# When the adaLN modulation halves end, who copies their result and when, and which engine makes two of their granules, in a one-core GLA + FNet layer

## The chip, the cores and the metric

The kernel runs on one core of a Trainium2 chip. The metric is device time in microseconds (us). Before the change the median of three runs is 1913.21 us (1912.01 to 1913.78).

The engines are named as the profile names them: PE is TensorE (PEld its weight loads), DVE is VectorE, ACT is ScalarE, POOL is GpSimd, SP is SyncE. Each takes its instructions in order from a queue of its own. A matmul writes to PSUM, and ScalarE or VectorE copy from there.

## The reference, cut to what matters

One inference step of one layer, on 128 context tokens and 256 latent tokens, 384 columns in all, with a model width of 2048:

```python
mod = silu(cond) @ w_ada + b_ada            # cond: c_ctx for context, c for latent tokens
sh1, sc1, ga1, sh2, sc2, ga2 = split(mod, 6)          # m = 0 .. 5
h = rmsnorm(x, norm_pre_mix) * (1 + sc1) + sh1
proj = h @ w_in                             # q | k | v | output gate | decay factors | Fourier channels
o = bidirectional_gla(q, k, v, decays)      # chunked scans, per-head RMSNorm, SiLU gate
f = real(fft2(fourier_channels))            # per group, over positions and channels
g_a, g_b = split(sigmoid(h @ w_gate + b_gate), 2)
m = (g_a * (o @ w_br_gla) + g_b * (f @ w_br_four)) @ w_out
x = x + ga1 * rmsnorm(m, norm_post_mix)
h = rmsnorm(x, norm_pre_ffn) * (1 + sc2) + sh2
x = x + ga2 * rmsnorm((silu(h @ w_ffn_gate) * (h @ w_ffn_up)) @ w_ffn_down, norm_post_ffn)
```

The change is about `mod` alone, and in it about m = 2, 3 and 4 (ga1, sh2, sc2), which are first needed late: ga1 in the output projection `w_out`, sh2 and sc2 behind it. There are only two condition vectors, so `mod` is a product of a 2048 x 2 matrix with very large weights, 2048 columns for each m.

## The kernel before

**Matmuls.** All is fp32. A weight tile of 128 x 1024 comes by a DMA of SP's queue (`raw`), and is then split into a high part `whi` (a cast, ScalarE, in `split`, L275) and a low part `wlo` (`raw` minus `whi`, VectorE, L295). The data are split likewise (`A_hi`, `A_lo`; `split_act`, L385, with VectorE's half in L387). `gemm` (L330; its matmul is L334) then issues 24 matmuls for one weight tile: for each of eight 128-row blocks the products `A_hi`·`whi`, `A_lo`·`whi` and `A_hi`·`wlo`, 128x384 each, into the PSUM tile `pmm`. Weight tiles for the Fourier channels are first folded by two VectorE operations into `ws` (L248, L249).

**The order on each engine** is the order in which the Python program emits instructions; nothing is rearranged around the change. Beside the main loops run generators, each advanced by one `yield` after every gemm (`step`, L326). One gemm with what is emitted behind it is called a step. The stages, in order:

- *GLA stage*: the projections q and k and the gates of `w_gate` (`proj`, L356, two steps each). `side()` of L1013 advances the GLA generator `gl` (L819: its matmuls write `dl`, `po` and others through L828, its states are `S`) and then the modulation generator.
- *Fourier stage* (`run_after`, L1093): modulation only at three turns.
- *Output-gate units* (`proj` with `gcol`, L1234, which gives `gs`, then `o`): `side()` of L1220 advances modulation at some turns, then the second Fourier transform (its PSUM tiles are `pp` and `pe`, its split results `edT` and `d`), then the Nyquist weights. Between units stand pieces of the Fourier branch projection, `four` (L1267), whose matmuls are `pf<-edT,whi` (L1281) and `pf<-edT,wlo` (L1282).
- *GLA branch projection*: for each i in `TAIL` one modulation step ahead of the gemm. Its end is `gate` times `pmm` (L1338).
- *w_out stage* (L1402 to L1433): 32 gemms with `wout` behind every second (squares and products into `qs`, by ScalarE and VectorE), modulation through `paced` (L374), which advances the generator as often as the sum of `rate[0]` passes a whole number; at `i == KT - 4` whatever is left is emitted at once. Behind this stage stand the row sums with `prow`, then the feed-forward network, which takes more than half of the time.

**Modulation.** m = 2, 3, 4 are made in six halves of 1024 columns by `ada_rest` (L730). A half has 16 granules, one for each block of 128 rows (the sixth leaves its last to the code behind `w_out`). Each granule is one step: POOL issues the load of a 128x1024 tile `adaw` (two buffers), and VectorE multiplies it by the two condition columns of `spad` and adds it into `adacc`, a tile of 2 x 1024 a partition, by two operations (L749; the first granule of a half, which has nothing to add to, by L747). Then the sum over the 128 partitions is taken on TensorE, the *selection*: `ada_select` (L722, matmul in L725), four matmuls for the first column and then four for the second, against a selector `selr`, into the PSUM tile `pr`. ScalarE copies `pr` to `adev` (L691). One step later two transposes (L695) turn it into `ptm`, and VectorE copies that into `mods` (L704) and adds the bias (L709), for some m multiplies too (L712).

A half's steps before the change: 16 granules, the last followed by one more empty `yield` (L757); then the selection and the copy to `adev`; then the transposes with VectorE's copies, and in the same step the first granule of the next half. That is 18 steps from half to half.

**Two granules on TensorE.** In the output-gate units turns 0 to 6 and turn 8 of `side()` carry a granule as described. At turns 9 and 13 the flag `on_pe` is set: there `ada_granule` (L716) makes the granule with four matmuls of its own (L718), straight from `adaw` and `spad` into `pr`, which is opened early for this and stays open until the half's selection, in the w_out stage.

Of the kernel before, what the change touches and what calls it, by code (L numbers as in the profile page):

```python
# [21 lines left out]
P = 128  # L22
# [16 lines left out]
XU = 1  # L39
GF = 25  # L40
GD = 256
TAIL = {4: False, 8: False, 10: False, 11: False, 13: False, 14: False}


C_TRI = 0
# [63 lines left out]
def tile_step(ctx: ExitStack, tc: tile.TileContext, a, o):  # L109
# [576 lines left out]

    adap = ctx.enter_context(tc.tile_pool(name="adap", bufs=1))

    def ada_tail(pr, m, half):
        ev = adap.tile([P, 256], F32, tag="adev", name="adev")  # L690
        ACT.copy(ev, pr)  # L691
        yield
        pt = pss.tile([P, 2, P], F32, tag="side", name="ptm")
        for b in range(2):
            PE.transpose(pt[:, b, :], ev[:, b * P : (b + 1) * P], ident)  # L695

        ada_out(DVE.tensor_copy, pt, m, half)
        ada_mods(m, half)

    def ada_out(copy, pt, m, half):  # L700
        src = pt.rearrange("p b (j r) -> p j b r", r=32)
        mh = mods[:, m, 8 * half : 8 * half + 8, :]
# [8 lines left out]
        if w1 is not None:  # L711
            DVE.tensor_mul(mh, mh, bc(norms[:, w1, :]))  # L712

    on_pe, ada_left = [False], []

    def ada_granule(pr, w, k, opened):  # L716
        for j in range(4):
# [10 lines left out]
                )  # L728

    def ada_rest(todo):  # L730
        for m, half in todo:
            acc = adap.tile([P, 2, 1024], F32, tag="adacc", name="adacc")
            pr, fresh = None, True
            final = (m, half) == todo[-1]
            for k in range(KT - final):
                w = adap.tile([P, 1024], F32, tag="adaw", name="adaw", bufs=2)
                POOL.dma_start(w, a["w_ada"][m - 2, half, k])
                if on_pe[0]:
                    opened = pr is not None
                    if not opened:  # L740
                        pr = pss.tile([P, 256], F32, tag="side", name="pr")
                    ada_granule(pr, w, k, opened)
                    yield
                    continue
                for c in range(2):
                    if fresh:
                        DVE.tensor_scalar_mul(acc[:, c, :], w, spad[:, k, c : c + 1])  # L747
                    else:
                        DVE.scalar_tensor_tensor(  # L749
                            acc[:, c, :], w, spad[:, k, c : c + 1], acc[:, c, :], op0=ALU.mult, op1=ALU.add,  # L750
                        )
                fresh = False
                yield
            if final:
                ada_left.append(acc)
                return
            yield  # L757
            opened = pr is not None
            if not opened:
                pr = pss.tile([P, 256], F32, tag="side", name="pr")  # L760
            ada_select(pr, acc, opened)
            yield from ada_tail(pr, m, half)

    def over_ends(k, t, r):

# [367 lines left out]
    with ExitStack() as s:  # L1133
# [85 lines left out]

        def side():  # L1220
            while True:
                on_pe[0] = turn[0] in (9, 13)
                if turn[0] < 7 or turn[0] in (8, 9, 13):
                    next(ada_gen, None)
                on_pe[0] = False
                turn[0] += 1
                next(df, None)
                next(nw, None)
                yield
# [72 lines left out]
        for b, i in mix_order:  # L1302
            if b == "o":
                if i == 1:
                    gate_of()
                proj(psm, hT, lambda p, i=i: gcol(p, i), sd, [lambda n=n: four(n) for n in between[i]])
                if i == 1:
                    gate_of()
                continue
            if b == "b":  # L1310
                if not i:
                    for g in (df, nw):
                        for _ in g:
                            pass
                    depth[0] = 4
                    spare_raws.extend([
                        lambda: px.tile([P, G], F32, tag="wr", name="raw3"), lambda: px.tile([P, G], F32, tag="cd", name="raw3"),
                    ])
                if not any(i in x for x in between):
                    four(i)  # L1320
            else:
                catch_up()
                if mT is None:
                    mT = alloc_A()
                if i == KT - 3:
                    depth[0] = 2
                    spare_raws.clear()
                if i in TAIL:
                    on_pe[0] = TAIL[i]
                    next(ada_gen, None)  # L1330
                    on_pe[0] = False
                p = psm.tile([P, T], F32, tag="mm", name="pmm")
                w = grab()
                while unstored:
                    unstored.pop()()
                gemm(p, w, oT, 8)
                g, y = gates.pop((b, i))
                DVE.tensor_mul(g, g, p)  # L1338
                DVE.tensor_add(y, y, g)
                if late:  # L1340
                    split_act(*late.pop())
                late.append((mT[0][:, i, :], mT[1][:, i, :], y))
                gate_of()
# [8 lines left out]
    with ExitStack() as s:  # L1352
# [44 lines left out]
            ACT.activation(sq2, mg32(i), AF.Square)  # L1397
            return sq0, pr, sq2

        rate[0] = 0.9  # L1400
        spare_h = {-4: ((pe, "hid_hi", 1), (pe, "hid_lo", 1)), -2: ((pe, "S0", 1), (pe, "S1", 1))}
        spare_w = ((adap, "adaw", 2), (adap, "adaw", 2))  # L1402
        for i in range(KT):
# [755 lines left out]
```

## Time and profile before

| what | value |
| --- | --- |
| median of three runs | 1913.21 us |
| the profiled execution, as timed | 1912.95 us |
| its span, first to last instruction | 1910.8 us |
| mean granted TensorE clock | 0.999 |
| ScalarE, GpSimd busy | 1002.2 us (52%), 82.7 us (4%) |
| HBM traffic over the span | 198 GB/s |

How to read the profile's lines: the first lists for each engine the busy time, its share of the span and the number of instructions. The chain of work that ended last is followed back from the last instruction, at each step to what released it; its line gives each engine's share. A line by stretches ("130.00:440.00") holds the length of the stretch, then busy time and instructions for PE, PEld, DVE, ACT and POOL, then the granted clock, the DMA share and GB/s. A line of the timeline holds the start in us, the time from the start of the first to the end of the last instruction in the group, the engine, the line of the code, the operation, what it writes and reads by the program's names, and how many; in square brackets the idle time of the engine before it, in us, and what ended it. Matmuls overlap in TensorE, so the next group can start before the last has ended. "issue" in the chain is time in which an engine waited for nothing that the profile shows.

### The profile page before, as it was taken

The numbers are of one execution on the slowest core, as the hardware profiler recorded it, in microseconds if no ns is written. First come the engines' busy times: TensorE is split into PE (matmuls) and PEld (weight loads), VectorE is DVE, ScalarE is ACT, GpSimd is POOL, SyncE is SP. The second block draws the span as 40 slices with busy tenths as digits, with TensorE's granted clock in tenths as the row PEclk, the third lists the DMA queues.
The fourth block names the chain that finished last, engine by engine and source line by source line (L and its number), as shares of the span: only waits on it lengthen the run. The fifth ranks groups of instructions, "written<-read, shape, count | busy, mean of one in ns | idle before, by whom it ended". The sixth has DMA issues, their size and how long they took to land.

```text
span 1910.8 us, 27279 instructions
## 1 busy us (share of the span) xinstructions
PE 1894.6 (99%) x10282; PEld 1675.1 (88%) x10282; DVE 1654.6 (87%) x2170; ACT 1002.2 (52%) x1430; POOL 82.7 (4%) x146
## 2 busy tenths in 40 slices
PE   8999999999999999999999999999999999999998
PEld 5679999999999999999988888888888888888886
DVE  5669897889969899998788989998999889997886
ACT  4235445444456654446456465646564656465644
POOL 0001111101000000004000000000000000000000
PEclk9999999999999999999999999999999999999999
DMA  9976766866657887666255656464646464746344
GB/s 390 400 278 232 262 225 225 274 205 211 216 176 233 278 288 260 206 219 221 67 186 152 188 147 202 135 213 116 223 129 219 119 219 116 232 106 199 95 159 138
DMA packets 237864, 389.70 MB, mean 204 GB/s; under 512 B 51188, under 2 KB 163924, under 8 KB 233380
## 3 DMA queue, kind: packets, MB, share of 16 engines
q1 hardware_dynamic: 218500, 330.02, 52.4%
q0 software_dynamic: 13952, 50.39, 8.6%
q10 hardware_dynamic: 5280, 7.55, 1.1%
q8 instruction: 81, 1.33, 0.3%
q14 instruction: 51, 0.42, 0.1%
HBM read 361.94 MB, written 16.78 MB: 198 GB/s over the span
## 4 chain that ended last, share of the span: by engine, by line
PE 95%; DMA 2%; DVE 2%; ACT 1%; issue 0%; SPq 0%; DVEq 0%; ACTq 0%
PE pmm L334 33%; PE pgu L346 31%; PE pdn L346 18%; PE pv L514 3%; PE pgm L497 1%; DMA slab<-in_w_ada 1%; PE pf L1281 1%; PE pfo L1083 1%; PE pmm L1561 1%; PE pf L1282 1%; PE po L828 1%; PE pfo L1084 0%; PE px L532 0%; DMA raw<-in_w_d 0%; DVE x1b L2016 0%; PE dl L828 0%
## 5 line engine op out<-in xcount | busy, mean ns | idle before, releaser
L334 PE MATMUL pmm<-A_hi,whi 128*128 128x384 f32 x1088 | 366.6, 337 | 0.0
L334 PE MATMUL pmm<-A_hi,wlo 128*128 128x384 f32 x1088 | 364.2, 335 | 0.1
L334 PE MATMUL pmm<-A_lo,whi 128*128 128x384 f32 x1088 | 363.9, 334 | 0.0
L1708 ACT CAST whi<-u 128x1024 fp32r<-128x1024 f32 x200 | 210.2, 1053 | 212.7 <-DVE u L1718 82.5
L1708 ACT CAST whi<-raw 128x1024 fp32r<-128x1024 f32 x175 | 184.0, 1051 | 169.7 <-DMA raw<-in_w_g 51.6
L1719 DVE TENSOR_TENSOR wlo<-u,whi 128x1024 fp32r<-128x1024 f32 x200 | 244.0, 1220 | 26.8 <-ACT whi L1708 21.4
L346 PE MATMUL pgu<-whi,A_lo 128*128 128x512 f32 x640 | 249.0, 389 | 0.0
L346 PE MATMUL pgu<-whi,A_hi 128*128 128x512 f32 x640 | 249.0, 389 | 0.0
L1719 DVE TENSOR_TENSOR wlo<-raw,whi 128x1024 fp32r<-128x1024 f32 x175 | 213.3, 1219 | 21.9 <-ACT whi L1708 12.3
L295 DVE TENSOR_TENSOR wlo<-raw,whi 128x1024 fp32r<-128x1024 f32 x161 | 196.2, 1219 | 29.6 <-ACT whi L308 29.1
L308 ACT CAST whi<-raw 128x1024 fp32r<-128x1024 f32 x147 | 154.3, 1050 | 123.5 <-DMA raw<-in_w_out 46.8
L749 DVE SCALAR_TENSOR_TENSOR adacc<-adaw,spad,adacc 128x1024 f32<-128x1024 f32 x174 | 215.3, 1278 | 0.7 <-DMA adaw<-in_w_ada 0.5
L334 PEld LDWEIGHTS pmm<-A_hi,whi 128*128 128x128 f32 x1088 | 204.2, 188 | 2.9 <-issue 1.7
L334 PEld LDWEIGHTS pmm<-A_hi,wlo 128*128 128x128 f32 x1088 | 204.2, 188 | 0.7 <-DVE wlo L295 0.6
L334 PEld LDWEIGHTS pmm<-A_lo,whi 128*128 128x128 f32 x1088 | 204.4, 188 | 0.2
L346 PE MATMUL pdn<-whi,hid_hi 128*128 128x512 f32 x480 | 186.8, 389 | 0.0
L346 PE MATMUL pdn<-whi,hid_lo 128*128 128x512 f32 x480 | 186.7, 389 | 0.0
L346 PE MATMUL pgu<-wlo,A_hi 128*128 128x512 f32 x640 | 184.0, 389 | 0.0
L346 PEld LDWEIGHTS pgu<-whi,A_lo 128*128 128x128 f32 x640 | 120.2, 188 | 25.0
L346 PEld LDWEIGHTS pgu<-wlo,A_hi 128*128 128x128 f32 x640 | 120.1, 188 | 25.0
L346 PEld LDWEIGHTS pgu<-whi,A_hi 128*128 128x128 f32 x640 | 120.1, 188 | 24.9
L346 PE MATMUL pgu<-whi,S 128*128 128x512 f32 x480 | 128.3, 389 | 0.0
(413 smaller groups left out, 3064.3 us busy)
## 6 DMA issues: line engine op xcount, KB each, us to landing
adaw<-in_w_ada POOLq DMA_DIRECT2D x95, 512.0 KB, 3.9
raw<-in_w_d SPq DMA_DIRECT2D x88, 512.0 KB, 3.9
slab<-in_w_ada SPq DMA_DIRECT2D x32, 1024.0 KB, 10.5
raw<-in_w_gate SPq DMA_DIRECT2D x64, 512.0 KB, 4.3
raw<-in_w_u SPq DMA_DIRECT2D x47, 512.0 KB, 3.8
raw<-in_w_in SPq DMA_DIRECT2D x46, 512.0 KB, 4.4
raw<-in_w_g SPq DMA_DIRECT2D x46, 512.0 KB, 3.6
u<-in_w_u SPq DMA_DIRECT2D x40, 512.0 KB, 4.5
```

The lines of the kernel that those rows point to most:

```text
L295: eng.tensor_sub(lo, raw, hi.bitcast(F32))
L308: ACT.copy(hi, raw)
L334: PE.matmul(dst, w[wi][:, k * n + n0 : k * n + n0 + P], x[xi][:, k0 + k, :], start=first and k == 0 and j == 0, stop=last and k == kts - 1 ...
L346: PE.matmul(dst, stat[x_][m], mov(w[w_], m), start=first and w_ == m == x_ == 0, stop=last and w_ == m == 1,)
L497: PE.matmul(pgv[q : q + 32, :], spad[:, k, :], slab[k // (KT // 2)][:, k % (KT // 2), :], start=k < 4, stop=k >= KT - 4,)
L514: PE.matmul(pv[2 * t + g], hT[x_][:, kb, t * P : (t + 1) * P], w_[:, g * 512 : (g + 1) * 512], start=kb == 0 and j == 0, stop=kb == KT - 1 ...
L749: DVE.scalar_tensor_tensor(acc[:, c, :], w, spad[:, k, c : c + 1], acc[:, c, :], op0=ALU.mult, op1=ALU.add,)
L828: PE.matmul(dst, w[wi], x[xi], start=first and j == 0, stop=last and j == 2)
L1083: PE.matmul(p, w_of[0][:, i, k, g, :], x[:, :, lo:hi], start=kt == 0, stop=False)
L1281: PE.matmul(pf[:, 0 : 2 * HT], w[0][:, c], x[k], start=k == 0, stop=False)
L1708: ACT.copy(hi, src)
L1719: DVE.tensor_sub(lo, src, hi.bitcast(F32))
```

## The change

1. **The halves end one step sooner.** The empty `yield` behind the 16th granule is gone: the selection and ScalarE's copy come one step after the last granule, at the place where the empty step was. So 17 steps lead from half to half, and each later half begins one step sooner than the one before.
2. **The copies come a step behind the transposes.** The transposes stay one step behind the selection, in the step of the next half's first granule. VectorE's copies into `mods` and the arithmetic on them are put into `finish()`, which is called one step later still, ahead of the next half's second granule.
3. **VectorE makes all granules.** Turns 9 and 13 of the output-gate units carry nothing, `on_pe` is gone, and so is the flag in `TAIL` (which was false throughout). `pr` is opened only at the selection. `ada_granule` stays for the last granule behind `w_out`. Since two steps fewer carry granules there and each half needs one step less, the places where later halves begin and end move by several steps.
4. **The pace in the w_out stage** is 0.85 instead of 0.9.

```diff
-TAIL = {4: False, 8: False, 10: False, 11: False, 13: False, 14: False}
+TAIL = (4, 8, 10, 11, 13, 14)
...
-    def ada_tail(pr, m, half):
-        ev = adap.tile([P, 256], F32, tag="adev", name="adev")
-        ACT.copy(ev, pr)
-        yield
-        pt = pss.tile([P, 2, P], F32, tag="side", name="ptm")
-        for b in range(2):
-            PE.transpose(pt[:, b, :], ev[:, b * P : (b + 1) * P], ident)
-
-        ada_out(DVE.tensor_copy, pt, m, half)
-        ada_mods(m, half)
...
     def ada_rest(todo):
+        finish = None
         for m, half in todo:
             acc = adap.tile([P, 2, 1024], F32, tag="adacc", name="adacc")
-            pr, fresh = None, True
             final = (m, half) == todo[-1]
             for k in range(KT - final):
                 w = adap.tile([P, 1024], F32, tag="adaw", name="adaw", bufs=2)
                 POOL.dma_start(w, a["w_ada"][m - 2, half, k])
-                if on_pe[0]:
-                    opened = pr is not None
-                    if not opened:
-                        pr = pss.tile([P, 256], F32, tag="side", name="pr")
-                    ada_granule(pr, w, k, opened)
-                    yield
-                    continue
+                if k and finish:
+                    finish()
+                    finish = None
                 for c in range(2):
-                    if fresh:
+                    if k == 0:
                         DVE.tensor_scalar_mul(acc[:, c, :], w, spad[:, k, c : c + 1])
...
-                fresh = False
                 yield
             if final:
                 ada_left.append(acc)
                 return
+            pr = pss.tile([P, 256], F32, tag="side", name="pr")
+            ada_select(pr, acc, False)
+            ev = adap.tile([P, 256], F32, tag="adev", name="adev")
+            ACT.copy(ev, pr)
             yield
-            opened = pr is not None
-            if not opened:
-                pr = pss.tile([P, 256], F32, tag="side", name="pr")
-            ada_select(pr, acc, opened)
-            yield from ada_tail(pr, m, half)
+            pt = pss.tile([P, 2, P], F32, tag="side", name="ptm")
+            for b in range(2):
+                PE.transpose(pt[:, b, :], ev[:, b * P : (b + 1) * P], ident)
+
+            def finish(pt=pt, m=m, half=half):
+                ada_out(DVE.tensor_copy, pt, m, half)
+                ada_mods(m, half)
...
         def side():
             while True:
-                on_pe[0] = turn[0] in (9, 13)
-                if turn[0] < 7 or turn[0] in (8, 9, 13):
+                if turn[0] < 7 or turn[0] == 8:
                     next(ada_gen, None)
-                on_pe[0] = False
...
                 if i in TAIL:
-                    on_pe[0] = TAIL[i]
                     next(ada_gen, None)
-                    on_pe[0] = False
...
-        rate[0] = 0.9
+        rate[0] = 0.85
```

**The first half's end, on TensorE.** In the GLA stage, between the gemms' matmuls, stand the two groups of `dl` for the two directions of the first head, and the selection (`pr<-adacc,selr`). Before:

```order
L334 MATMUL pmm<-A_hi,wlo 128x384
L828 MATMUL dl<-vr,part 128x256 x6
L334 MATMUL pmm<-A_hi,whi 128x384
...
L334 MATMUL pmm<-A_hi,wlo 128x384
L828 MATMUL dl<-vr,part 128x256 x6
L725 MATMUL pr<-adacc,selr 32x256 x8
L334 MATMUL pmm<-A_hi,whi 128x384
```

After, with the transposes into `ptm` (from `adev`) at the end:

```order
L334 MATMUL pmm<-A_hi,wlo 128x384
L818 MATMUL dl<-vr,part 128x256 x6
L714 MATMUL pr<-adacc,selr 32x256 x8
L334 MATMUL pmm<-A_hi,whi 128x384
...
L334 MATMUL pmm<-A_hi,wlo 128x384
L818 MATMUL dl<-vr,part 128x256 x6
L748 MATMUL ptm<-ident,adev 128x128 x2
L334 MATMUL pmm<-A_hi,whi 128x384
```

The selection has moved from behind the second group of `dl` to behind the first, one gemm of 24 matmuls sooner. Everything emitted ahead of it, on every engine, stands as before. The selections of the second, third and fourth half move by two, three and four steps in the same way.

**The output-gate units, on VectorE.** Here the first granules of the fifth half were made; `gs`, `o_lo`, `d` and `ws` are the unit's own. Before:

```order
L387 TENSOR_TENSOR o_lo<-gs,o_hi 128x384
L387 TENSOR_TENSOR d_5539<-pe,d_5539 128x194 x2
L248 TENSOR_TENSOR ws<-raw 128x512
L249 TENSOR_TENSOR ws<-raw 128x512
L704 COPY mods<-ptm 128x8 x2
L709 TENSOR_TENSOR mods<-mods,cols_b 128x16
L747 TENSOR_SCALAR adacc<-adaw,spad 128x1024 x2
L1240 SCALAR_TENSOR_TENSOR gs<-gs,gnorm,pt 128x384
L295 TENSOR_TENSOR wlo<-ws,whi 128x1024
```

After:

```order
L387 TENSOR_TENSOR o_lo<-gs,o_hi 128x384
L734 SCALAR_TENSOR_TENSOR adacc<-adaw,spad,adacc 128x1024 x2
L387 TENSOR_TENSOR d_5551<-pe,d_5551 128x194 x2
L248 TENSOR_TENSOR ws<-raw 128x512
L249 TENSOR_TENSOR ws<-raw 128x512
L734 SCALAR_TENSOR_TENSOR adacc<-adaw,spad,adacc 128x1024 x2
L1228 SCALAR_TENSOR_TENSOR gs<-gs,gnorm,pt 128x384
L295 TENSOR_TENSOR wlo<-ws,whi 128x1024
```

The fourth half's copies and the fifth's first granule have moved up and out of these rows, and two later granules of the fifth half stand there now.

**The fifth half's end, on VectorE.** In the w_out stage `qs`, `sq` and the 128x384 `pr` belong to `wout`. Before:

```order
L1388 TENSOR_TENSOR qs<-qs,sq 128x384
L749 SCALAR_TENSOR_TENSOR adacc<-adaw,spad,adacc 128x1024 x2
L295 TENSOR_TENSOR wlo<-raw,whi 128x1024
L749 SCALAR_TENSOR_TENSOR adacc<-adaw,spad,adacc 128x1024 x2
L295 TENSOR_TENSOR wlo<-raw,whi 128x1024
L1384 TENSOR_TENSOR qs<-qs,sq 128x384
L1386 TENSOR_TENSOR pr<-Bhi,Chi 128x384
L1387 TENSOR_TENSOR qs<-qs,pr 128x384
L1388 TENSOR_TENSOR qs<-qs,sq 128x384
L749 SCALAR_TENSOR_TENSOR adacc<-adaw,spad,adacc 128x1024 x2
L295 TENSOR_TENSOR wlo<-raw,whi 128x1024 x2
```

After:

```order
L1374 TENSOR_TENSOR qs<-qs,sq 128x384
L734 SCALAR_TENSOR_TENSOR adacc<-adaw,spad,adacc 128x1024 x2
L295 TENSOR_TENSOR wlo<-raw,whi 128x1024 x2
L1370 TENSOR_TENSOR qs<-qs,sq 128x384
L1372 TENSOR_TENSOR pr<-Bhi,Chi 128x384
L1373 TENSOR_TENSOR qs<-qs,pr 128x384
L1374 TENSOR_TENSOR qs<-qs,sq 128x384
L732 TENSOR_SCALAR adacc<-adaw,spad 128x1024 x2
L295 TENSOR_TENSOR wlo<-raw,whi 128x1024 x2
```

The fifth half's last granule, the lowest of the three before, is now the first row of its kind; the sixth half's first granule (L732) follows two steps behind. The selection on TensorE has moved up by three gemms.

More of the change, by code (lines that the diff above doesn't have):

```diff
@@ L712, in ada_mods @@
             DVE.tensor_mul(mh, mh, bc(norms[:, w1, :]))
-    on_pe, ada_left = [False], []
+    ada_left = []
     def ada_granule(pr, w, k, opened):
```

## The prediction

> **What bounds the kernel now.** I read the page first: the busy times, then the chain of work that ended last.
>
> ```profile
> PE 1894.6 (99%) x10282; PEld 1675.1 (88%) x10282; DVE 1654.6 (87%) x2170; ACT 1002.2 (52%) x1430; POOL 82.7 (4%) x146
> PE 95%; DMA 2%; DVE 2%; ACT 1%; issue 0%; SPq 0%; DVEq 0%; ACTq 0%
> ```
>
> TensorE (PE) is busy nearly throughout and makes up 95% of the chain. So the change can only act through TensorE: by work taken from it, or by a pause put into it. Next, busy times by stage, over the stretches in which modulation work is placed, and TensorE's waits in them.
>
> ```profile
> core 0: us, PE busy (x) PEld busy (x) DVE busy (x) ACT busy (x) POOL busy (x), PEclk, DMA share, GB/s
> 130.00:440.00 310.00, 310.00 (x1991) 305.39 (x1991) 269.93 (x339) 152.45 (x258) 34.11 (x67) 1.00 0.71 239
> 440.00:536.00 96.00, 95.90 (x644) 94.12 (x642) 89.21 (x132) 46.47 (x76) 5.94 (x11) 1.00 0.68 217
> 536.00:690.00 154.00, 154.00 (x975) 149.61 (x968) 130.39 (x239) 93.69 (x152) 5.30 (x10) 1.00 0.71 237
> 690.00:731.00 41.00, 41.00 (x244) 41.00 (x244) 40.59 (x60) 17.31 (x30) 2.65 (x5) 1.00 0.85 289
> 731.00:860.00 129.00, 129.00 (x756) 128.13 (x755) 117.73 (x139) 62.38 (x99) 10.07 (x19) 1.00 0.64 218
> PEld pmm L334 <- DVE wlo L295: 0.6, 2, 0.4
> ```
>
> TensorE has no idle stretch here, and its waits for VectorE's weight parts come to 0.6 us. VectorE (DVE) is the second fullest: 269.93 of 310 us in the first stretch and 40.59 of 41 in the fourth, so what it is given comes out late, though nobody waits for that now.
>
> **The first half's selection.** A modulation half is 16 granules on VectorE, then the selection on TensorE, then two transposes. Before, one empty step (a step is 24 matmuls of L334 and what is put behind them) stood between the last granule and the selection. It is gone: the selection moves to behind the first group of dl matmuls. Where it goes and what it waits for, from the timeline of VectorE and of TensorE, the price of a handover in the chain, and the granules' loads on the page:
>
> ```profile
> 210.71 2.48 DVE L749 SCALAR_TENSOR_TENSOR adacc<-adaw,spad,adacc 128x1024 f32<-128x1024 f32 x2
> 209.85 0.88 PE L828 MATMUL dl<-vr,part 128*128 128x256 f32 x6
> 210.57 0.34 PE L334 MATMUL pmm<-A_hi,whi 128*128 128x384 f32 x1
> 215.56 1.07 PE L725 MATMUL pr<-adacc,selr 128*32 128x256 f32 x16
> 216.56 0.45 PE L334 MATMUL pmm<-A_hi,whi 128*128 128x384 f32 x1
> 866.32 0.14 issue
> adaw<-in_w_ada POOLq DMA_DIRECT2D x95, 512.0 KB, 3.9
> ```
>
> The row at 210.71 is the last granule; it ends at 213.19. TensorE reaches the selection's new place at 210.57. The selection takes 1.00 us (215.56 to 216.56) in two parts: the first needs the granule's first operation, the second its second. Unhindered it would end at 211.57. As it is, the second part starts at 213.19 plus a handover of 0.14 (the chain's "issue" between VectorE's r and the matmuls of prow) and takes 0.50: end at 213.83, so **+2.3 us**. Bounds: 2.1 without the handover, 2.8 if the whole selection has to wait. Nothing on any engine is moved before this place, so these times stand. Behind the waiting selection TensorE's whole queue stands, the next 24 matmuls first; ScalarE's copy of the result stands behind a cast that waits for VectorE's S anyway. The granules' loads move with them on POOL's queue, the next one issued when a buffer of two comes free and landed 3.9 us later, within the step of 24 matmuls that lies between: 0, and without that cover the granule, and with it the selection, would come up to 3.9 us later. On SP's queue two neighbouring weight loads change places at the start of the output-gate units, with whole steps still ahead of their first use: 0.
>
> **The second, third and fourth.** Each half ends one step sooner than the last did, so the n-th last granule stands n-1 steps earlier and its selection n steps. At these places stand now:
>
> ```profile
> 291.15 2.47 DVE L749 SCALAR_TENSOR_TENSOR adacc<-adaw,spad,adacc 128x1024 f32<-128x1024 f32 x2
> 292.18 0.88 PE L828 MATMUL po<-part,qp 128*128 128x256 f32 x6
> 292.89 0.33 PE L334 MATMUL pmm<-A_hi,whi 128*128 128x384 f32 x1
> 369.14 2.47 DVE L749 SCALAR_TENSOR_TENSOR adacc<-adaw,spad,adacc 128x1024 f32<-128x1024 f32 x2
> 374.85 0.34 PE L334 MATMUL pmm<-A_hi,whi 128*128 128x384 f32 x1
> 534.10 2.47 DVE L749 SCALAR_TENSOR_TENSOR adacc<-adaw,spad,adacc 128x1024 f32<-128x1024 f32 x2
> 540.38 0.38 PE L1169 MATMUL pp<-cd,X 128*128 128x129 f32 x2
> ```
>
> Second: granule to 293.62, plus 0.64 gives 294.26, against 293.89 unhindered (292.89 + 1.00): **+0.4**. The pause before it moves both engines here; if VectorE follows less, nothing is left, and if it has its one additional granule not yet worked off, 2.5 more are due: bounds 0 and 2.9. Third: granule to 371.61, due at 374.85: 3.2 us of cover. Fourth: to 536.57, due at 540.38: 3.8 us. Both cost **0**; without that cover each would cost like the first. The waits of 0.6 us between 440 and 536 can vanish when TensorE comes later: **-0.3**, bounds 0 and -0.6.
>
> **The two granules of TensorE.** Rows around one of them, and the same place in a unit without:
>
> ```profile
> 602.67 0.34 PE L334 MATMUL pmm<-A_hi,wlo 128*128 128x384 f32 x1
> 602.94 0.64 PE L718 MATMUL pr<-adaw,spad 128*32 128x256 f32 x8
> 603.81 0.42 PE L1281 MATMUL pf<-edT,whi 128*128 128x388 f32 x1
> 616.90 0.34 PE L334 MATMUL pmm<-A_hi,wlo 128*128 128x384 f32 x1
> 617.32 0.42 PE L1281 MATMUL pf<-edT,whi 128*128 128x388 f32 x1
> ```
>
> From the last gemm matmul to pf it is 1.14 us with a granule and 0.42 without: 0.72 each, **-1.44** for both (the eight matmuls overlap: 0.64 us in all). VectorE pays in the same units. Its rows there, and the margin of a weight part:
>
> ```profile
> 573.56 0.68 DVE L249 TENSOR_TENSOR ws<-raw 128x512 f32<-128x512 f32 x1
> 576.03 0.24 DVE L704 COPY mods<-ptm 128x8 f32<-128x8 f32 x2 [1.79 <-PE ptm L695]
> 576.40 1.41 DVE L747 TENSOR_SCALAR adacc<-adaw,spad 128x1024 f32<-128x1024 f32 x2
> 601.40 1.22 DVE L295 TENSOR_TENSOR wlo<-ws,whi 128x1024 fp32r<-128x1024 f32 x1
> 604.08 0.25 PE L1282 MATMUL pf<-edT,wlo 128*128 128x194 f32 x1
> 688.37 0.56 DVE L1338 TENSOR_TENSOR gate<-gate,pmm 128x384 f32<-128x384 f32 x1 [0.77 <-PE pmm L334]
> ```
>
> Between ws and the next gs, the wait for ptm (1.79), the copies and the half-price first granule (576.03 to 577.81) become one granule of 2.48, with another of 2.48 ahead of d: from 574.24, 3.57 us become about 4.8, so VectorE is some 1.25 us later from here. wlo is done at 602.62 and used at 604.08: 1.46 us of margin, which the lateness (1.25) and TensorE's earliness (0.72) together exceed. So part of the 1.44 is waited away in these units; not all before 688.37, where VectorE's 0.77 us of idleness absorbs some lateness.
>
> **The fifth selection** settles what is left of it. It moves three steps up, to behind the matmuls that end before this row:
>
> ```profile
> 746.95 2.48 DVE L749 SCALAR_TENSOR_TENSOR adacc<-adaw,spad,adacc 128x1024 f32<-128x1024 f32 x2
> 747.02 0.33 PE L334 MATMUL pmm<-A_hi,whi 128*128 128x384 f32 x1
> ```
>
> Last granule to 749.43, plus 0.64: 750.07, against 748.02 unhindered: **+2.05**. This end is VectorE's: whatever TensorE gained before, it waits here that much longer, since VectorE at 99% from 690 to 731 does not follow. So of the -1.44 I count 0 (bounds 0 and -1.44), and VectorE's own shift, from -0.8 (688.37's idleness used up) to +1.25, I take at +0.2. ACT's copy behind this selection fills idle time. The rate of 0.85 for 0.9 only sets which steps carry granules; the last of them end about a step earlier than now, behind TensorE's matmuls: 0. Copying mods a step later removes waits of VectorE alone: 0; without spare VectorE time they would be worth 1.79 here.
>
> Sum: 2.3 + 0.4 - 0.3 + 2.05 + 0.2 = **+4.6 us** on the profiled execution's 1912.95 (span 1910.8), that is 1917.6; it lies 0.26 under the median of 1913.21, so 1917.8 for a median. Bounds: 2.1 + 0 - 0.6 + 1.9 - 0.8 = 2.6 and 2.8 + 2.9 + 2.2 + 1.25 = 9.2; the upper needs every worst at once, and I end my own case at +6.8: 1915.8 to 1920.0.
>
> What a pause does to the clock: the end of the trace.
>
> ```profile
> 1901.52 1.13 PE L2005 MATMUL py<-ep,psums 128*128 128x128 f32 x8 [1.82 <-ACT r L1981]
> 1903.36 1.06 PE L2005 MATMUL py<-ep,psums 128*128 128x128 f32 x8
> 1900.00:1905.00 5.00, 2.90 (x24) 2.73 (x24) 4.59 (x19) 3.34 (x9) 0.20 (x1) 1.00 0.75 219
> 1905.00:1911.00 6.00, 0.00 (x0) 0.00 (x0) 1.48 (x5) 0.00 (x0) 0.00 (x0) 0.62 0.58 167
> ```
>
> A pause of 1.82 us left the granted clock at 1.00. After the last matmul (to 1904.42) it fell: a mean of 0.62 over 6 us is full speed for 1.4 us and half after, a fall at 1906.4, some 2.0 us into the idleness. My pauses of 2.1 to 2.5 lie just above both, so the rows allow a drop. [...]
>
> **The rivals.** *VectorE is in time* (not slower): decided at 210.57, 292.89 and 747.02, where it would have to be 2.3, 0.4 and 2.05 us earlier against TensorE than reckoned. For it: its waits for ptm go. Against: nothing is moved ahead of the first place. Then only the granules count: -1.44, 1911.8. *VectorE becomes the bound*: its lateness of 1.25 in the output-gate units is not worked off and the second selection meets the additional granule; decided by the margin of 1.46 us at 604.08. For it: 40.59 of 41. Against: 0.77 idle at 688.37. Then +2 to +3 more: 1920 to 1921. *The clock drops in the pauses*: half speed for at least the 2 us that it took to fall costs 1 us or more each, two pauses 2 to 4: 1920 to 1922. It is decided by a pause over 2.0 us.
>
> **How the numbers follow.** My case 0.73, VectorE in time 0.12, VectorE the bound 0.10, the clock 0.05. Predicted 1917.8. The range 1914.8 to 1920.6 leaves out the first rival, the upper ends of the others and little of my case. What a measurement of this kernel can tell from no change is about 0.2%, 3.8 us: 1909.4 to 1917.0. Over it: most of my case and the two later rivals, 0.58. Within: the rest of my case and the first rival, 0.39. Under 1909.4 nothing leads: 0.03.
>
> **What would show it.** In the changed profile: before the first and fifth selections' second parts TensorE idle by about 2 us each, released by VectorE's adacc; under 1 us at the second, none at the third and fourth; no L718 between 560 and 680, and pf 0.72 sooner behind gemm; the gain gone by 760. Wrong would be: no idle time before selr matmuls, idle time before wlo of more than 2 us in all, or a granted clock under 1.00 before 1900.

## The result and the profile after

The changed kernel takes 1924.64 us (median of 6 runs, 1922.74 to 1928.13) against 1912.91 us before (6 runs, 1912.01 to 1913.78). The ratio is 1.0065, 95% interval 1.0052 to 1.0078: slower by 11.7 us, where 4.6 were forecast. Its profiled execution was the slowest of the six, 1928.13 us with a span of 1926.4. The six fall into groups by their granted clock: 1922.74 at 0.999, 1924.39 to 1927.36 at 0.997 and 0.998, 1928.13 at 0.996. So there is something in it that does not happen each time, and it shows in the clock.

The chain of work that ended last, and the stretches that were shown of before:

```profile
PE 86%; DVE 7%; DMA 3%; issue 1%; ACT 1%; SPq 0%; DVEq 0%; ACTq 0%
core 0: us, PE busy (x) PEld busy (x) DVE busy (x) ACT busy (x) POOL busy (x), PEclk, DMA share, GB/s
130.00:440.00 310.00, 306.67 (x1953) 300.99 (x1953) 270.06 (x335) 147.35 (x250) 35.57 (x70) 0.99 0.71 237
440.00:536.00 96.00, 95.34 (x586) 94.62 (x586) 90.38 (x134) 47.74 (x77) 5.92 (x11) 1.00 0.69 216
536.00:690.00 154.00, 151.82 (x991) 145.68 (x990) 129.53 (x231) 91.57 (x149) 4.75 (x9) 1.00 0.70 229
690.00:731.00 41.00, 41.00 (x247) 41.00 (x247) 39.78 (x66) 20.85 (x36) 1.58 (x3) 1.00 0.88 284
731.00:860.00 129.00, 125.81 (x720) 124.17 (x719) 110.23 (x133) 54.21 (x88) 10.04 (x19) 0.97 0.63 215
```

VectorE has gone from 2% of the chain to 7%: TensorE now waits for it. TensorE stands idle for 3.3 us in the first stretch and for 3.2 in the last, where it had no idle time before, and in these same two stretches the clock is below 1.00. In the output-gate units (536 to 690) it is idle for 2.2 us.

The first half's last granule on VectorE, the selection on TensorE (now L714), and the matmuls behind it:

```profile
212.09 2.48 DVE L734 SCALAR_TENSOR_TENSOR adacc<-adaw,spad,adacc 128x1024 f32<-128x1024 f32 x2
209.81 0.87 PE L818 MATMUL dl<-vr,part 128*128 128x256 f32 x6
213.48 0.64 PE L714 MATMUL pr<-adacc,selr 128*32 128x256 f32 x8 [2.79 <-issue]
214.62 1.08 PE L714 MATMUL pr<-adacc,selr 128*32 128x256 f32 x8 [0.51 <-DVE adacc L734]
215.63 0.69 PE L334 MATMUL pmm<-A_hi,whi 128*128 128x384 f32 x1
216.12 0.52 PE L334 MATMUL pmm<-A_lo,whi 128*128 128x384 f32 x1
220.60 0.44 PE L334 MATMUL pmm<-A_hi,whi 128*128 128x384 f32 x1
220.88 0.34 PE L334 MATMUL pmm<-A_lo,whi 128*128 128x384 f32 x1
```

There are two losses here. TensorE is done with `dl` at 210.68 and has the selection behind it at 215.70: 5.02 us for 1.00 us of work, 4.0 more than unhindered. Of these, 3.30 us are idle time (2.79 and 0.51); the rest is the selection itself, whose two parts no longer overlap and whose second part takes 1.08 us instead of 0.64. And the matmuls behind it take 0.52 us each instead of 0.34, until 220.6. The granted clock over these stretches, and over the same of the fifth half:

```profile
213.50:214.00 0.50, 0.50 (x8) 0.13 (x8) 0.50 (x1) 0.00 (x0) 0.00 (x0) 0.99 0.89 344
214.00:220.50 6.50, 5.99 (x27) 5.07 (x24) 5.24 (x9) 1.62 (x3) 0.53 (x1) 0.50 0.87 316
220.50:221.00 0.50, 0.50 (x3) 0.50 (x3) 0.12 (x1) 0.00 (x0) 0.00 (x0) 0.68 0.00 0
760.00:760.50 0.50, 0.14 (x4) 0.00 (x0) 0.50 (x1) 0.00 (x0) 0.00 (x0) 0.63 0.00 0
760.50:766.50 6.00, 5.80 (x23) 4.99 (x24) 2.51 (x3) 1.31 (x2) 0.53 (x1) 0.50 0.62 206
```

The clock (third number from the end) is at 0.50 from 214.0 to 220.8 and from 760.1 to 767.0. The fifth selection looks like the first, and the chain in order of time shows what the half clock costs: 24 matmuls of L334 in another unit, then those behind the fifth selection.

```profile
759.51 0.64 PE L714 MATMUL pr<-adacc,selr 128*32 128x256 f32 x8 [2.64 <-DVE adacc L734]
760.70 1.08 PE L714 MATMUL pr<-adacc,selr 128*32 128x256 f32 x8 [0.56 <-DVE adacc L734]
642.58 4.20 PE pmm L334 x24
761.78 6.75 PE pmm L334 x24
```

6.75 instead of 4.20: 2.55 us at each of the two places. In the output-gate units TensorE waits for VectorE's weight parts and for `o_lo`; the longest two:

```profile
612.63 0.36 PE L1270 MATMUL pf<-edT,wlo 128*128 128x194 f32 x1 [1.06 <-DVE wlo L295]
660.92 0.45 PE L334 MATMUL pmm<-o_lo,whi 128*128 128x384 f32 x1 [0.74 <-DVE o_lo L387]
```

How far the same matmuls of TensorE have shifted between the two profiled executions:

| matmul | before | after | shift |
| --- | --- | --- | --- |
| first `po` behind the first selection | 220.83 | 227.41 | 6.6 |
| a `pt` early in the output-gate units | 575.83 | 583.21 | 7.4 |
| a `pf` at their end | 651.72 | 661.38 | 9.7 |
| first row sum behind the w_out stage | 860.80 | 876.78 | 16.0 |

So 6.6 us are lost at the first selection, 0.8 from there to the units (0.2 of it at the second selection), 2.3 in the units and 6.3 at the fifth selection.

### The profile page after: what moved, and what is told of

Same layout as the page of the kernel before. It is cut to its first block, busy times and chain, and to the rows that moved or that the text cites. A ratio compares the mean times of both kernels' runs of the same rounds, so it can differ in the third digit from the quotient of the medians.

```text
span 1926.4 us, 27259 instructions
## 1 busy us (share of the span) xinstructions
PE 1901.8 (99%) x10266; PEld 1679.7 (87%) x10266; DVE 1659.2 (86%) x2174; ACT 1002.7 (52%) x1430; POOL 82.4 (4%) x146
## 4 chain that ended last, share of the span: by engine, by line
PE 86%; DVE 7%; DMA 3%; issue 1%; ACT 1%; SPq 0%; DVEq 0%; ACTq 0%
PE pgu L346 31%; PE pmm L334 26%; PE pdn L346 18%; PE pv L514 3%; DVE adacc L734 2%; DVE wlo L295 1%; PE pgm L497 1%; DMA slab<-in_w_ada 1%; PE pmm L1547 1%; PE pfo L1073 1%; PE pf L1269 1%; PE po L818 1%; PE px L532 0%; DMA raw<-in_w_br_gla 0%; DMA raw<-in_w_d 0%
## 5 line engine op out<-in xcount | busy, mean ns | idle before, releaser
L334 PE MATMUL pmm<-A_hi,whi 128*128 128x384 f32 x1088 | 369.0, 339 | 0.0
L334 PE MATMUL pmm<-A_hi,wlo 128*128 128x384 f32 x1088 | 366.1, 336 | 0.7 <-DVE wlo L295 0.7
L334 PE MATMUL pmm<-A_lo,whi 128*128 128x384 f32 x1088 | 365.8, 336 | 0.0
L734 DVE SCALAR_TENSOR_TENSOR adacc<-adaw,spad,adacc 128x1024 f32<-128x1024 f32 x178 | 220.2, 1278 | 0.8 <-DMA adaw<-in_w_ada 0.5
L334 PEld LDWEIGHTS pmm<-A_hi,whi 128*128 128x128 f32 x1088 | 205.8, 189 | 3.7 <-issue 3.3
L334 PEld LDWEIGHTS pmm<-A_hi,wlo 128*128 128x128 f32 x1088 | 205.6, 189 | 1.4 <-DVE wlo L295 1.3
L334 PEld LDWEIGHTS pmm<-A_lo,whi 128*128 128x128 f32 x1088 | 206.0, 189 | 0.2
```

Source lines behind the costliest of these rows:

```text
L334: PE.matmul(dst, w[wi][:, k * n + n0 : k * n + n0 + P], x[xi][:, k0 + k, :], start=first and k == 0 and j == 0, stop=last and k == kts - 1 ...
L734: DVE.scalar_tensor_tensor(acc[:, c, :], w, spad[:, k, c : c + 1], acc[:, c, :], op0=ALU.mult, op1=ALU.add,)
```

## The experiments

Theory A: what is lost is the two waits at the first and the fifth selection, and the half clock behind each. Theory B: the two granules that VectorE took over make it the bound, and the waits only show it. Each kernel was timed in turns with the kernel before, whose medians are 1913.07 us beside the first four kernels below, 1913.30 beside the next three and the last, and 1913.41 beside the three on the length of a wait.

### The empty step back in every half

Of the kernel after, VectorE making all granules, the copies a step late:

```diff
+            yield
             pr = pss.tile([P, 256], F32, tag="side", name="pr")
             ada_select(pr, acc, False)
...
-        rate[0] = 0.85
+        rate[0] = 0.97
```

> The kernel after, with the empty step restored between the last granule and the selection of every half (pace in the w_out stage 0.97, since two granules more are left for it). Theory A (TensorE waits at the first and fifth selection, 4.1 and 3.7 us, and each wait is followed by some 6.5 us at half clock, 2.5 us more): both waits and the half clock go, granted clock 0.999; what stays is VectorE's lateness in the output-gate units (2.3 us net), 1912.9 + 2.3 = 1915.2, range 1913 to 1916.5. Theory B (the two granules that VectorE took over make it the bound, the waits at the selections only show it): the time stays at 1920 or more, with TensorE's waits turning up before weight parts instead.

1912.83 us (11 runs), ratio to before 0.9998 (0.9989 to 1.0006): the whole 11.7 us are gone, the granted clock is 0.999. Theory B falls. The 2.3 us of the units that I expected to stay went too (0.25 us of idle time there), so the time lies just below the range of 1913 to 1916.5. What TensorE gained by two granules less is given back at the fifth selection:

```profile
215.97 1.07 PE L714 MATMUL pr<-adacc,selr 128*32 128x256 f32 x16
768.11 0.64 PE L714 MATMUL pr<-adacc,selr 128*32 128x256 f32 x8 [0.36 <-DVE adacc L734]
769.31 0.64 PE L714 MATMUL pr<-adacc,selr 128*32 128x256 f32 x8 [0.56 <-DVE adacc L734]
```

The first selection runs through in 1.07 us, without a wait. The fifth waits, but for 0.36 and 0.56 us, and ends 1.2 us later than unhindered.

### The empty step alone taken away

One line of the kernel before:

```diff
                 return
-            yield
             opened = pr is not None
```

> The kernel before with one line less: the empty step ahead of the selection. TensorE keeps its two granules, the pace stays 0.9. Theory A: the first selection waits as in the kernel after (3 to 5 us in all, half clock behind it), the fifth likewise if VectorE is behind there: 1919 to 1925, granted clock 0.996 to 0.998. Theory B: no more than the kernel before with the waits that its VectorE has time for, 1912 to 1915.

1921.62 us (5 runs), ratio 1.0044 (1.0031 to 1.0056), clock 0.997 in the profiled execution. This line alone makes most of the loss, with TensorE's granules as they were: theory A. At the first selection:

```profile
213.30 0.64 PE L725 MATMUL pr<-adacc,selr 128*32 128x256 f32 x8 [2.25 <-issue]
214.45 1.08 PE L725 MATMUL pr<-adacc,selr 128*32 128x256 f32 x8 [0.51 <-DVE adacc L749]
205.00:225.00 20.00, 17.24 (x97) 15.78 (x97) 15.62 (x26) 6.79 (x14) 1.59 (x3) 0.83 0.66 231
```

A wait of 2.25 us was enough for the half clock (0.83 over the 20 us around). The fifth selection fell on another step here and waited 1.0 us in two pieces, without half clock.

### VectorE makes all granules, nothing else

The kernel before, with

```diff
-                on_pe[0] = turn[0] in (9, 13)
-                if turn[0] < 7 or turn[0] in (8, 9, 13):
+                if turn[0] < 7 or turn[0] == 8:
...
-        rate[0] = 0.9
+        rate[0] = 0.97
```

> The kernel before with its 18 steps from half to half, but VectorE makes the two granules of turns 9 and 13 later (pace 0.97); copies right behind the transposes. Theory A: no wait at any selection; TensorE is rid of 1.3 us, VectorE's lateness in the units costs 0 to 2.3: 1912 to 1915. Theory B: 1919 or more. It differs from gap_all only in the place of the copies of mods: if that place counts, the two differ by over 1 us.

1913.08 us (11 runs), ratio 1.0 (0.9991 to 1.0009). The granules' move costs nothing and brings nothing that this can measure. It differs from the kernel with all empty steps (1912.83) only in the place of the copies, so that place is worth nothing measurable either.

### The empty step back in two halves only

```diff
+            if (m, half) in (todo[0], todo[4]):
+                yield
             pr = pss.tile([P, 256], F32, tag="side", name="pr")
             ada_select(pr, acc, False)
...
-        rate[0] = 0.85
+        rate[0] = 0.92
```

> The kernel after, with the empty step restored in the first and the fifth half only (pace 0.92). Theory A: the second, third and fourth selection cost under 0.5 us each, as in the kernel after, so 1913 to 1916.5, clock 0.999. Theory B: 1920 or more. If every half needs its empty step, idle time stands before the second to fourth selections here: 1916 to 1920.

1916.05 us (11 runs), ratio 1.0014 (1.0005 to 1.0023), clock 0.999. No selection waits, and of the 11.7 us 8.6 are gone. What is left stands for the most part in the output-gate units, where TensorE is idle for 2.4 us, against 2.2 in the kernel after (the next expectation puts the 2.4 at 2.6).

### One granule less in the units

The last kernel, with

```diff
-                if turn[0] < 7 or turn[0] == 8:
+                if turn[0] < 5 or turn[0] in (6, 8):
...
-        rate[0] = 0.92
+        rate[0] = 0.96
```

> gap_1_5 with one granule less in the output-gate units (turn 5 carries none, pace 0.96). gap_1_5 took 1916.05, with 2.6 us of TensorE's waits for wlo and o_lo in these units, in which VectorE makes 13 granule operations where the kernel before makes 11. If their number is the cause, the waits shrink to under 1 us and the time to 1913.3 to 1915. If the shifted place of the copies or the missing granules of TensorE is the cause, it stays at 1916.

1914.43 us (11 runs), ratio 1.0007 (0.9998 to 1.0015): 1.6 us less for one granule less. The place in the units where TensorE waited longest, first with, then without that granule; the columns are as in the timelines above:

```profile
606.85 0.36 PE L1272 MATMUL pf<-edT,wlo 128*128 128x194 f32 x1 [1.08 <-DVE wlo L295]
```

```profile
604.40 0.36 PE L1272 MATMUL pf<-edT,wlo 128*128 128x194 f32 x1
```

The wait is gone at the same instruction, and TensorE's idle time in the units falls from 2.4 to 1.0 us. So the granules that fall into the units are what makes TensorE wait there. Counted from the first `pp`, at two operations for a granule, VectorE starts 11 granule operations in these units in the kernel before and in the two kernels with 18 steps from half to half, 14 in the kernel after, 13 in the one before this one, 11 here. With the same 11, this kernel is idle for 1.0 us there and the one with all empty steps for 0.25, so the granules' places count too. The steps that were saved had been filled with granules, in a stage where VectorE had no room for them.

### The wait filled with matmuls

The kernel after, with matmuls in front of two selections, whose result the selection overwrites:

```diff
             pr = pss.tile([P, 256], F32, tag="side", name="pr")
+            if (m, half) in (todo[0], todo[4]):
+                x = hT if (m, half) == todo[0] else mT
+                for _ in range(22):
+                    PE.matmul(pr, x[0][:, 0, 0:P], x[0][:, 0, 0:256], start=True, stop=True)
             ada_select(pr, acc, False)
```

> The kernel after, with 22 matmuls of 128x256 put in front of the selection of the first and the fifth half (into the same PSUM tile, which the selection then overwrites), so that TensorE works through most of the wait instead of standing idle. The selections still end when VectorE lets them. If the idleness is what halves the clock, the half clock goes (granted clock 0.999) and the time falls by about 2.9 us for each of the two places, from 1924.6 to 1918.5, range 1917.5 to 1920. If the half clock has another cause, or costs nothing because VectorE is the bound behind it, the time stays within 1 us of 1924.6.

1920.59 us (5 runs), ratio 1.0037 (1.0025 to 1.005), clock 0.999 to 1.0 in each run. TensorE has more to do and the kernel is 4.0 us faster, because the clock stays up:

```profile
213.59 0.64 PE L714 MATMUL pr<-adacc,selr 128*32 128x256 f32 x8 [0.17 <-DVE adacc L734]
214.78 0.64 PE L714 MATMUL pr<-adacc,selr 128*32 128x256 f32 x8 [0.56 <-DVE adacc L734]
205.00:225.00 20.00, 19.27 (x133) 18.17 (x132) 18.19 (x28) 7.18 (x14) 2.11 (x4) 1.00 0.78 268
```

The selection starts no sooner than in the kernel after (213.59 against 213.48), since VectorE sets its time. The half clock comes from the idleness, and without it the median is 4.0 us lower. Not all of this need be the clock: at the fifth selection VectorE was 2.9 us behind in this profile and 3.95 in that of the kernel after. The 4.0 are less than the 6.1 that I had expected from the profiled execution (1920.59 lies just above the range of 1917.5 to 1920), which was the slowest of its six and had it at both places.

### TensorE makes the last granule of two halves

```diff
-                for c in range(2):
+                for c in range(0 if k == KT - 1 and (m, half) in (todo[0], todo[4]) else 2):
...
+            on_pe = (m, half) in (todo[0], todo[4])
+            if on_pe:
+                ada_granule(pr, w, KT - 1, False)
-            ada_select(pr, acc, False)
+            ada_select(pr, acc, on_pe)
```

> The kernel after, with TensorE making the last granule of the first and the fifth half by four matmuls in front of the selection; VectorE has one granule less there, so the selection needs only VectorE's 15th, a step older. If the two waits and what follows them are the loss, they shrink from 6.6 and 6.3 us (the profiled execution) to about 0.7 plus a few tenths each: 1924.6 - 11 = 1913.5 to 1917, clock 0.999, with the 2.3 us of the output-gate units left. If VectorE is the bound in any case, 1920 or more.

1916.75 us (11 runs), ratio 1.0018 (1.0009 to 1.0027), clock 0.999. With the selection at its early place, but not in need of VectorE's last granule, the shift behind the first selection is 0.7 us instead of 6.6. That is the four matmuls. The fifth selection runs through without a wait too. Of the 3.5 us that are left against the kernel before, 2.2 are idle time in the units.

### How long a wait brings the half clock

The filled kernel with 6 matmuls, with 12 in the same way, and the kernel after once more, unchanged.

```diff
-                for _ in range(22):
+                for _ in range(6):
```

> As filled, with 6 matmuls instead of 22: each shortens the idle time by 0.12 us, so TensorE stands idle for some 2.0 us before the first part of the selection instead of 2.7. If half clock follows any pause over about 2 us, it comes in some executions: clock 0.997 to 0.999, 1920.5 to 1924. If only pauses of 2.6 us and more do it, clock 0.999 and 1920.6 as filled.

> As filled, with 12 matmuls: some 1.3 us idle. The end of the kernel before stood idle for 1.82 us with the clock staying at 1.00, so no half clock: 0.999, 1920.6 as filled. If the half clock comes here too, it is not the length of the pause alone that brings it.

> The kernel after, unchanged, for a second profile. Its six executions lay between 1922.74 (clock 0.999) and 1928.13 (0.996). If this spread is half clock at two, one or none of the two places, this profile's clock and its time go together: 0.999 with 1921 to 1923, 0.997 or 0.998 with 1924 to 1926, 0.996 with 1927 to 1928. If it is the landing of the weight tile at 144 us, the time goes with that landing instead.

With 6: 1922.62 us (4 runs, 1919.67 to 1924.17), ratio 1.0046 (1.0031 to 1.0061). The half clock came after 1.93 us of idleness, in the middle of the sparse matmuls of the selection. Around it the timeline, then the stretches of the clock:

```profile
213.42 0.92 PE L714 MATMUL pr<-adacc,selr 128*32 128x256 f32 x8 [1.93 <-DVE adacc L734]
214.62 1.08 PE L714 MATMUL pr<-adacc,selr 128*32 128x256 f32 x8 [0.28 <-DVE adacc L734]
213.20:213.60 0.40, 0.18 (x4) 0.16 (x8) 0.40 (x2) 0.00 (x0) 0.00 (x0) 1.00 0.55 184
213.80:217.00 3.20, 2.92 (x20) 1.58 (x13) 3.20 (x6) 0.00 (x0) 0.53 (x1) 0.50 0.92 320
217.20:217.40 0.20, 0.20 (x3) 0.20 (x2) 0.20 (x2) 0.00 (x0) 0.00 (x0) 1.00 0.70 287
```

With 12: 1920.47 us (5 runs), ratio 1.004 (1.0026 to 1.0055), with waits of 0.41 and 0.56 us at the first selection and no half clock in the profiled execution. The idle time expected here, 1.3 us, was not met, because VectorE's half ended 0.74 us sooner in that execution than in the profile of the kernel after; what 1.3 us do at this place stays open.

The kernel after again: 1924.51 us (4 runs, 1922.25 to 1928.68), ratio 1.0061 (1.0046 to 1.0076), and clock and time go together once more: 1922.25 at 0.999, 1924.49 and 1924.53 at 0.998, 1928.68 at 0.996. That one was profiled, and has the half clock at both places, for 6.8 us at the first and 3.4 at the fifth. It has it at a third place too, behind a wait of 1.78 us for a weight part. The landing of the weight tile at 144 us, the other explanation in the expectation, does not go with the time in the two profiles of this kernel: the cast behind it starts at 144.06 us here and at 144.24 in the first profile, which was 0.55 us faster. That the 6 us between the fastest and the slowest run are for the most part half clock is read from their clocks alone; the other three have no profile.

The third place, with the stretches around it:

```profile
465.18 0.44 PE L334 MATMUL pmm<-A_hi,wlo 128*128 128x384 f32 x1 [1.78 <-DVE wlo L295]
462.33:465.74 3.41, 1.63 (x11) 1.32 (x10) 3.38 (x5) 2.59 (x4) 0.00 (x0) 1.00 0.41 141
465.74:469.15 3.41, 3.41 (x13) 3.41 (x12) 3.38 (x8) 0.53 (x2) 0.00 (x0) 0.50 0.67 181
469.15:472.57 3.42, 3.42 (x23) 3.42 (x22) 3.38 (x6) 2.46 (x4) 0.00 (x0) 1.00 0.39 126
```

A wait of 1.78 us brought the half clock here, and the pause of 1.82 us at the end of the kernel before did not. So the length of a pause alone does not decide. The two stretches of the same length at that end, up to the fall at 1906.40:

```profile
1899.57:1902.99 3.42, 1.60 (x15) 1.50 (x14) 3.01 (x13) 2.35 (x5) 0.63 (x2) 1.00 0.88 258
1902.99:1906.40 3.41, 1.42 (x13) 1.23 (x11) 3.41 (x13) 1.14 (x4) 0.00 (x0) 1.00 0.60 170
```

TensorE is idle for 1.82 us in the first of them, which ends without a fall, and for 1.99 us in the second, which ends in one. In the kernel after, the 3.41 us ahead of the falls at 213.99 and 760.13 hold 2.79 and 2.63 us of idle time, and no other stretch between 9 and 1921 us, cut in the same length from the first of these falls, holds more than 1.47. What sets the moment of a fall was not shown.

### A second empty step in the fifth half

The kernel with all empty steps, plus

```diff
             yield
+            if (m, half) == todo[4]:
+                yield
...
-        rate[0] = 0.97
+        rate[0] = 1.0
```

> gap_all with a second empty step in the fifth half (pace 1.0, so that its last granule comes a step sooner while its selection stays where it is). gap_all's profile has a wait of 1.2 us at the fifth selection, which ate what the two granules taken from TensorE had gained. If that wait goes, 1911.6, range 1911 to 1912.6, which would be the fastest so far; if TensorE's gain is eaten elsewhere, 1912.8 as gap_all.

1911.90 us (11 runs), ratio 0.9993 (0.9984 to 1.0002). The last granule and the selection of the fifth half:

```profile
760.33 2.47 DVE L734 SCALAR_TENSOR_TENSOR adacc<-adaw,spad,adacc 128x1024 f32<-128x1024 f32 x2
767.20 1.07 PE L714 MATMUL pr<-adacc,selr 128*32 128x256 f32 x16
```

The 1.2 us that the fifth selection lost with all empty steps are gone: 4.4 us now lie between granule and selection. It is the fastest kernel here, and faster than the kernel after by more than 12 us; against the kernel before its 1.4 us are not told apart from no change.

## Why the prediction was wrong, step by step

The direction and the two places were right, the size was not: 4.6 us forecast, 11.7 measured, and 1924.64 lies above the range's 1920.6. Four steps failed:

- **"The clock drops in the pauses" was given 0.05.** It happened. TensorE's wait of 2.79 us at the first selection and of 2.64 at the fifth each brought half clock, 2.55 us more behind each in the profiled execution and about 4 us of the median (the filled kernel). The sum had nothing for it. The end of the trace of before had shown the fall about 2.0 us into the idleness; I set it aside on the assumption that a pause has to be longer, which no trace here shows. The measurement decides: idle time of 1.93, 2.25, 2.64 and 2.79 us was enough here. And I took this rival as one that stands in place of my own case, where it is added to it: the condition, "a pause over 2.0 us", was met by my own forecast of 2.1 to 2.5.
- **"Nothing on any engine is moved before this place, so these times stand"** (first selection, +2.3). It cost 4.0 us. The order stands, the times do not: they were those of one execution. VectorE's last granule ended 4.0 us after TensorE was at the place (210.53 and 214.57), where 2.6 were reckoned; the rest is the selection at half clock. From 145 to 213 us VectorE has hardly any slack (in every one of these profiles it stands idle for 0.96 us, for ScalarE), so it carries on whatever it starts with, and that is ScalarE's cast of a weight tile which lands between 143.3 and 144.3. The cast in the profile of before, and in that of the kernel with all empty steps, which is the same up to there:

```profile
143.29 1.05 ACT L308 CAST whi<-raw 128x1024 fp32r<-128x1024 f32 x1 [5.39 <-DMA raw<-in_w_in]
```

```profile
144.26 1.05 ACT L308 CAST whi<-raw 128x1024 fp32r<-128x1024 f32 x1 [5.81 <-DMA raw<-in_w_in]
```

  In the twelve profiles in which VectorE makes all of the first half, this half ends there between 213.19 and 214.73 us. That of before is the earliest, nine of the others lie from 214.09 on. In five of the twelve (these two among them) it ends 69.9 us after that cast starts. In the other seven it takes 0.2 to 0.7 us more, by a second wait for ScalarE, here in the kernel after; what makes ScalarE late there was not traced:

```profile
167.12 1.02 DVE L852 SCALAR_TENSOR_TENSOR la<-z,la 128x512 f32<-128x512 f32 x2 [0.46 <-ACT la L850]
```

  The bounds of 2.1 to 2.8 held the handover's size open, and not this.
- **"Of the -1.44 I count 0"** (the units). TensorE did not only lose the gain, it lost 2.3 us more (7.4 to 9.7 in the table of shifts). The margin of 1.46 us at the weight part was exceeded as reckoned; I had stopped there, with the thought that the fifth selection settles what is left. But the fifth selection settled nothing: it lost time of its own, and the 2.3 us came on top of it.
- **The fifth selection, +2.05**, cost 3.9 us: VectorE's last granule ended 3.95 us after TensorE was at the place (756.70 and 760.65), where 2.4 were reckoned. What VectorE had taken on in the units is not the cause, since VectorE stands idle for 2.33 us just ahead of its last two granules, for ScalarE's cast of a weight tile. That tile's load is issued 11.5 us before TensorE is at the place, before and after alike (735.51 and 745.20). From there to the cast it takes 3.7 us before and 5.2 after, and from the cast to the granule's end 10.23 us in both. The cast in the kernel before, in the kernel after and in that with 6 matmuls of filling, which has the same granules in the units:

```profile
739.20 1.05 ACT L308 CAST whi<-raw 128x1024 fp32r<-128x1024 f32 x1 [2.04 <-DMA raw<-in_w_out]
```

```profile
750.42 1.05 ACT L308 CAST whi<-raw 128x1024 fp32r<-128x1024 f32 x1 [4.00 <-DMA raw<-in_w_out]
```

```profile
748.57 1.05 ACT L308 CAST whi<-raw 128x1024 fp32r<-128x1024 f32 x1 [2.33 <-DMA raw<-in_w_out]
```

  With the last of them VectorE is 2.27 us late, about as reckoned. So here too the forecast took one execution's landing for fixed; why the load took longer stays open. With all empty steps the fifth selection costs 1.2, and with the granule a step ahead nothing.

Right were: the second selection (0.2 us lost, +0.4 forecast), the third and fourth without a wait, the copies' place worth nothing, and the granule loads' and the pace's zero. "VectorE in time" fell at 213.48. The waits of 440 to 536 did not vanish (-0.3): two of 0.20 and 0.46 us stand there still. "VectorE becomes the bound" holds in the units alone. Two of the signs named as wrong came: a granted clock under 1.00 before 1900, and 2.1 us of idle time before weight parts.

## What to carry to other kernels

An empty step between the last operation of one engine and the first that needs it on a full engine is slack, and where both engines are full it decides: look up how long the producer is behind at that place, in several executions and not in one. A wait of a full TensorE is priced with its wait and, where it leaves TensorE idle as long as the waits that brought it here (1.78 to 2.79 us), with the half clock that can follow. And steps that are saved in one place are work that comes sooner in another: look at what is full there.

## What the runs showed of the hardware that was not expected

- The half clock came after 1.78 us idle for a weight part (the kernel after again), 1.93 us idle with the selection's sparse matmuls behind it (6 matmuls of filling), 2.25 us (one line removed), and 2.64 and 2.79 us (the kernel after). A pause of 1.82 us at the end of the kernel before left the clock at 1.00, as did 0.41 and 0.56 us close together (12 matmuls of filling).
- The half clock lasted 3.4 us in some places (213.7 to 217.1 with 6 matmuls of filling, 465.74 to 469.15 in the kernel after again) and 6.8 us in others (214.0 to 220.8 and 760.1 to 767.0 in the kernel after). TensorE was at work in them but for 0.6 us at most. What decides between the two lengths was not shown.
- Filling two waits with useless matmuls made the kernel 4.0 us faster.
